# Attention scores scaled in their PSUM bank by the instruction that finds the row's extreme, in a two-group encoder layer

## The chip, the cores and the metric

The kernel runs on 1 core of one Trainium2 chip. The metric is the device time of one execution in microseconds (us), as a median of several runs. A core has a matrix engine (TensorE, PE in the profile; its weight loads are PEld), VectorE (DVE), ScalarE (ACT), GpSimd (POOL) and SyncE (SP). Here SP issues all DMA transfers, in one queue. PSUM is the memory that the matrix engine writes into; a "bank" below is a PSUM tile.

## The reference

Two request groups ("prompt" and "sample", 1024 tokens of 1024 channels each) go through the same layer, one after the other. Only what the change touches is shown: the scores are scaled by 1/8, a softmax is taken over 1024 keys, and at the end a gated residual is added to x.

```python
# branch A: 8 query heads, 2 key heads; branch B: 4 heads, two softmax maps each
qa = rms_norm(qa, qn_a); ka = rms_norm(ka, kn_a)         # per head, then rotary positions
s = einsum('bqgrd,bkgd->bgrqk', qblk, k) * scale         # scale = 1/sqrt(64)
p = softmax(s)                                            # over 1024 keys
oa = (p @ v) * silu(za)
p = softmax(s)                                            # branch B, maps m = 0, 1
pd = p[:, :, 0] - lam * p[:, :, 1]
ob = rms_norm(pd @ v, subln_g) * (1 - lam_init) * silu(zb)
merged = sigmoid(ga) * (oa @ w_proj_a) + sigmoid(gb) * (ob @ w_proj_b)
y = x + gate * (merged @ w_out)
```

The kernel gets x of both groups also transposed (`xT_prompt`, `xT_sample`) and writes y transposed.

## The kernel before

All matrices of weights are split into a high and a low part (`w[..., 0, :]`, `w[..., 1, :]`: ACT at L193 rounds, POOL at L195 subtracts), so a product takes three matmuls. For each group the program runs:

- `kva_gen`, `qa_gen`, `qkb_gen`, `vb_gen`: projections for keys, queries and values. `proj_tt` (L569) fills a bank `f` for a token tile of 128; ACT copies it into `row` (L584), `rms` takes sums of squares (L588, L589 on DVE) and a power of -0.5 (L590 on POOL), `rope` turns the positions (L613 to L619), and L630 transposes the row on PE.
- `z_gen` (L755, L763, L765): the gate paths; it fills PE between attention steps.
- `attention`: 64 units a run, four score tiles each, 256 tiles in all. `scores` calls `softmax_unit` for a tile of 128 queries by 1024 keys. PE writes it into a bank `s` (L789, L790; two 512-wide halves, two matmuls each). DVE takes the negated maximum of the raw row (L791) and multiplies it by `rs` (L792). `rs` is the query's inverse RMS: the queries are left unnormalised, and their norm comes in as the scale of the exponential. ACT then computes exp(rs * s + m) into a tile `p` with the row's sum (L793). `flip` transposes `p` in 32 by 32 blocks on DVE (L834); in branch B it first combines the two maps (L833, with a factor from L818 on DVE and L819 on POOL). Four DMAs bring the pieces to the right partitions of a tile `q` (L843), and `a_values` (L857) or `b_values` (L874) multiplies by the values on PE.
- `gated_gen` (L952, L962 to L964): loads attention outputs (`od`) back and applies the gates.
- `merge_gen` (L1029), then `out_gen` (L1064, L1069) for the first group and `out_seven` (L1136, L1174, a seven-product scheme) for the second. Both load rows of x (L1057, L1115, L1166) and add the product to them.

There are two `s` banks. So a score tile waits until the exponential of the tile two before it has read its bank. There are four `p` tiles and three `q` tiles.

The order on each engine is made at build time: the tile framework schedules all instructions by estimated durations, and steps of the attention get a higher priority (`high_priority(offset=AHEAD)`). The streams are mixed by `weave` with shares such as `Z_SHARE` and `ATT_W`. `behind(a, b)` adds a dependency without a wait: it only puts a after b in the order. An instruction that costs another estimate can therefore change the order of everything that is scheduled after it.

The 1/sqrt(64) of the scores (`SC`) is in the gain tables `gqa` and `gB`, made once (L434, L470).

Of the kernel before, what the change touches and what calls it, by code (L numbers as in the profile page):

```python
# [14 lines left out]
AF = mybir.ActivationFunctionType  # L15
ALU = mybir.AluOpType
# [4 lines left out]
P = 128  # L21
# [68 lines left out]
def kernel(ctx: ExitStack, tc: tile.TileContext, t: dict):  # L90
# [340 lines left out]
    def load_tables():  # L431
        for dst, src in ((gqa, "qn_a"), (gka, "kn_a")):
            dma(dst, t[src][0].partition_broadcast(P))
        nc.vector.tensor_scalar(out=gqa, in0=gqa, scalar1=SC, scalar2=None, op0=ALU.mult)  # L434

# [31 lines left out]
    def load_tables_B():  # L467
        for i, src in enumerate(("qn_b", "kn_b")):
            dma(gB[:, i, :], t[src][0].partition_broadcast(P))
        nc.vector.tensor_scalar(out=gB[:, 0, :], in0=gB[:, 0, :], scalar1=SC, scalar2=None, op0=ALU.mult)  # L470
        nc.vector.tensor_tensor(out=gB[:, 1, 16:], in0=gB[:, 1, 16:], in1=gB[:, 0, 16:], op=ALU.mult)
# [311 lines left out]
    def softmax_unit(q, sw, k, pt, su, rs):  # L783

        m = tiny.tile([P, 1], F32, tag="m", name=nm("m"))
        s = sbank()
        for n in range(2):
            sl = slice(n * 512, (n + 1) * 512)
            nc.tensor.matmul(s[:, sl], q, k[:, sl], start=True, stop=False)  # L789
            nc.tensor.matmul(s[:, sl], sw, k[:, sl], start=False, stop=True)  # L790
        nc.vector.tensor_reduce(out=m, in_=s, axis=AX.X, op=ALU.max, negate=True)  # L791
        nc.vector.tensor_tensor(out=m, in0=m, in1=rs, op=ALU.mult)  # L792
        nc.scalar.activation(  # L793
            pt.rearrange("p (j c a) -> p j c a", j=4, c=8), s.rearrange("p (c a j) -> p j c a", c=8, j=4),
            AF.Exp, bias=m, scale=rs, accum_out=su,
        )
# [137 lines left out]


    def gated_gen(st, i, hf, oT):

# [11 lines left out]
        for c in range(2):  # L949
            e = 2 * i + c  # L950
            o = rtile()
            dma(o, st["od"][e][hf])  # L952
            if e < 4:
# [95 lines left out]
    def out_gen(g, mT):  # L1049

        for eu in range(4):
            w = load_w(w_cols(w_out, (eu * 256, 256)))
            ys = halves(pair())
            for e in range(2):
                ec = eu * 2 + e
                y = ys[e]
                dma(y, xT_in[g][ec * P : (ec + 1) * P])  # L1057
                for hf in range(2):
# [46 lines left out]
    def out_seven(g, parts, md):  # L1105
# [4 lines left out]
        def open_pair(d, job):  # L1110
            job["w"] = load_seven(d)
            job["y"] = [ptile() for _ in range(2)]
            for e in range(2):
                ec = d + 4 * e
                dma(job["y"][e], xT_in[g][ec * P : (ec + 1) * P])  # L1115
            job["t"] = mtile("tab", [P, 512])
# [48 lines left out]
        for e in range(2):  # L1165
            dma(ys[e], xT_in[g][e * 512 : e * 512 + P])  # L1166
        sums = sums_of(parts, md)
# [215 lines left out]
```

## Time and profile before

| | |
|---|---|
| median of 3 runs | 1889.78 us (1889.75 to 1890.94) |
| the profiled execution | 1885.75 us, of which the span is 1884.0 us |
| TensorE busy | 1837.1 us (98% of the span), 10398 matmuls |
| VectorE busy | 1227.3 us (65%) |
| ScalarE busy | 777.3 us (41%) |
| GpSimd busy | 610.7 us (32%) |
| granted TensorE clock | 0.992 of full speed |

The span runs from the first to the last instruction. A group row of the profile gives line, engine, operation, output<-inputs and shapes, then the count, the busy time, the mean duration in ns, the engine's idle time just before these instructions, and what ended it. Matmuls are pipelined and their recorded ends are modelled, so their mean duration (396 ns at L755) is longer than the distance between two of them. A row of waits reads: who waited, for whom, us in total, how many times, the longest.

### The profile page before, as it was taken

The page shows a single profiled execution, that of the slowest core. Times are in us where ns is not written, and L with a number is a line of the kernel's source. Part 1 is how long each engine was busy: PE and PEld are TensorE (multiplying, and loading weights), DVE is VectorE, ACT ScalarE, POOL GpSimd, SP SyncE. Part 2 cuts the span into 40 slices and gives each one's busy share as a digit, 9 for nine tenths or more (in the row PEclk, how much of TensorE's full clock was granted, in tenths as well). Part 3 has the DMA queues.
Part 4 walks back from the last instruction along what each step waited for, and adds up shares of the span by engine and source line. Part 5 has one row for each costly group of instructions (what it writes and reads, how often), then busy time and mean ns, then how long its engine had stood idle before and what let it go on. Part 6 is the DMA issues. An engine that isn't in the chain of part 4 may idle for free.

```text
span 1884.0 us, 29900 instructions
## 1 busy us (share of the span) xinstructions
PE 1837.1 (98%) x10398; PEld 1552.8 (82%) x10398; DVE 1227.3 (65%) x2016; ACT 777.3 (41%) x1544; POOL 610.7 (32%) x888
## 2 busy tenths in 40 slices
PE   6999999999999999999999999999999999999999
PEld 3798878888899877888889887788888898888887
DVE  5777766454776777347466687665357856773795
ACT  4544434343554544213223444344344545442241
POOL 1343311442453452221233333014354635232100
PEclk7999999999999999999999999999999999999999
DMA  9135776564444467754631567666524443675442
GB/s 324 57 94 160 208 197 181 147 181 143 124 113 121 132 205 226 236 154 134 209 134 52 158 180 196 191 183 187 163 72 133 120 117 101 177 245 171 129 129 90
DMA packets 283895, 295.46 MB, mean 157 GB/s; under 512 B 41952, under 2 KB 236640, under 8 KB 283744
## 3 DMA queue, kind: packets, MB, share of 16 engines
q1 hardware_dynamic: 283744, 293.54, 53.1%
q8 instruction: 83, 1.36, 0.3%
q14 instruction: 68, 0.56, 0.1%
HBM read 133.98 MB, written 42.01 MB: 93 GB/s over the span
## 4 chain that ended last, share of the span: by engine, by line
PE 67%; issue 4%; DMA 4%; DVE 3%; POOL 3%; SPq 2%; ACT 1%; ACTq 0%; POOLq 0%; DVEq 0%
PE f L755 16%; PE f L569 14%; PE f L1029 7%; PE a L874 5%; PE s L789 4%; PE s L790 4%; PE a L857 3%; PE s L1029 3%; PE f L1064 3%; PE s L1064 2%; PE f L1136 2%; SPq L843 1%; PE s L1136 1%; DMA q<-p 1%; DMA st<-in_w_in_dram 1%
## 5 line engine op out<-in xcount | busy, mean ns | idle before, releaser
L755 PE MATMUL f<-u,w 128*128 128x512 f32 x2232 | 565.7, 396 | 1.0 <-POOL w L195 0.8
L755 PEld LDWEIGHTS f<-u,w 128*128 128x128 f32 x2232 | 410.5, 189 | 83.8 <-POOL w L195 1.8
L569 PE MATMUL f<-w,u 128*128 128x256 f32 x3456 | 472.7, 287 | 1.8 <-ACT row L584 0.6
L569 PEld LDWEIGHTS f<-w,u 128*128 128x128 f32 x3456 | 449.7, 192 | 23.2 <-issue 3.3
L791 DVE TENSOR_REDUCE m<-s 128x1 f32<-128x1024 f32 x256 | 309.4, 1217 | 104.4 <-PE s L790 102.4
L195 POOL TENSOR_TENSOR w<-st,w 128x512 fp32r<-128x512 f32 x160 | 214.1, 1356 | 394.5 <-ACT w L193 375.6
L834 DVE STREAM_TRANSPOSE p<-p 128x1024 f32<-128x1024 f32 x192 | 237.7, 1242 | 84.3 <-ACT p L793 68.2
L793 ACT ACTIVATE p<-s,m,u 128x1024 f32<-128x1024 f32 x128 | 153.9, 1204 | 164.8 <-issue 71.1
L790 PE MATMUL s<-u,sw 128*128 128x512 f32 x512 | 201.5, 398 | 0.0
L793 ACT ACTIVATE p<-s,m,rsB 128x1024 f32<-128x1024 f32 x128 | 153.8, 1203 | 107.2 <-DVE m L792 88.1
L193 ACT ACTIVATE w<-st 128x512 fp32r<-128x512 f32 x184 | 107.4, 626 | 99.5 <-DMA st<-in_w_in_dram 85.7
L1029 PE MATMUL f<-u,w 128*128 128x512 f32 x552 | 131.1, 392 | 0.0
L874 PE MATMUL a<-q,u 128*128 128x256 f32 x512 | 125.1, 381 | 2.8 <-DMA q<-p 1.9
L857 PE MATMUL a<-q,u 128*64 128x256 f32 x1024 | 117.9, 382 | 5.5 <-DMA q<-p 4.9
L1029 PEld LDWEIGHTS f<-u,w 128*128 128x128 f32 x552 | 103.0, 188 | 21.1
L590 POOL TENSOR_TENSOR rsB<-ss,nhalf 128x4 f32<-128x4 f32 x64 | 65.9, 1031 | 150.9 <-DVE ss L589 132.9
L633 DVE TENSOR_TENSOR u<-f,u 64x256 fp32r<-64x256 f32 (+1 forms) x198 | 81.4, 411 | 48.6 <-ACT u L632 43.3
L763 ACT ACTIVATE ev<-f 128x512 f32<-128x512 f32 x93 | 55.2, 594 | 139.0 <-PE f L755 90.3
L790 PEld LDWEIGHTS s<-u,sw 128*128 128x128 f32 x512 | 96.7, 189 | 16.8 <-issue 0.4
L789 PE MATMUL s<-u 128*128 128x512 f32 x256 | 107.6, 425 | 2.9 <-ACT p L793 2.9
L874 PEld LDWEIGHTS a<-q,u 128*128 128x128 f32 x512 | 94.7, 190 | 17.9 <-issue 3.3
L857 PEld LDWEIGHTS a<-q,u 128*64 128x64 f32 x1024 | 76.3, 137 | 40.0 <-issue 10.3
(221 smaller groups left out, 2181.6 us busy)
## 6 DMA issues: line engine op xcount, KB each, us to landing
q<-p SPq DMA_DIRECT2D x768, 128.0 KB, 2.6
st<-in_w_in_dram SPq DMA_DIRECT2D x132, 256.0 KB, 3.2
zd<-ev SPq DMA_DIRECT2D x96, 256.0 KB, 2.6
sw<-u SPq DMA_DIRECT2D x256, 64.0 KB, 2.0
u<-in_w_ada_dram SPq DMA_DIRECT2D x8, 1024.0 KB, 11.4
oo<-zd SPq DMA_DIRECT2D x64, 128.0 KB, 2.3
od<-oo SPq DMA_DIRECT2D x64, 128.0 KB, 2.4
st<-in_w_in_dram SPq DMA_DIRECT2D x64, 128.0 KB, 2.7
```

Of the source, the lines that this page charges most:

```text
L193: nc.scalar.activation(wh, st, AF.Copy)
L195: e.tensor_tensor(out=wl, in0=st, in1=wh.bitcast(F32), op=ALU.subtract)
L569: ins = nc.tensor.matmul(ps, lt[c][:, sl], w[:, c, wi, :], start=(k == 0), stop=(k == 23))
L755: ins = nc.tensor.matmul(ps, w[:, c, wi, e * P : (e + 1) * P], rt[c], start=(k == 0), stop=(k == 23),)
L789: nc.tensor.matmul(s[:, sl], q, k[:, sl], start=True, stop=False)
L790: nc.tensor.matmul(s[:, sl], sw, k[:, sl], start=False, stop=True)
L791: nc.vector.tensor_reduce(out=m, in_=s, axis=AX.X, op=ALU.max, negate=True)
L793: nc.scalar.activation(pt.rearrange("p (j c a) -> p j c a", j=4, c=8), s.rearrange("p (c a j) -> p j c a", c=8, j=4), AF.Exp, bias=m, scal ...
L834: nc.vector.transpose(pt, pt)
L857: lambda k=k, m=m: nc.tensor.matmul(acc[(LO, HI)[m]], u["v"][:, k], pT[m][:, k], start=(k == 0), stop=(k == 7))
L874: nc.tensor.matmul(acc, u["v"][:, k], pT[:, k], start=(k == 0), stop=(k == 7))
L1029: nc.tensor.matmul(ps, w[:, c, wi, d * P : (d + 1) * P], o[:, oi, :], start=(k == 0), stop=(k == 11))
```

## The change

In `softmax_unit`, one VectorE instruction takes the place of two. It multiplies the bank by `rs` in place, takes the minimum with 3.0e38 (which changes nothing), and gives the row's minimum as an accumulator output. The gain tables carry -SC in place of SC, so the bank holds negated scores and the minimum is the negated maximum. The exponential then has the constant scale -1.0 and only its bias is read for each row.

The second part: rows of x in `out_gen` and `out_seven` are put behind the last load of an attention output in `gated_gen` by `behind`.

```diff
-        nc.vector.tensor_scalar(out=gqa, in0=gqa, scalar1=SC, scalar2=None, op0=ALU.mult)
+        nc.vector.tensor_scalar(out=gqa, in0=gqa, scalar1=-SC, scalar2=None, op0=ALU.mult)
...
-        nc.vector.tensor_scalar(out=gB[:, 0, :], in0=gB[:, 0, :], scalar1=SC, scalar2=None, op0=ALU.mult)
+        nc.vector.tensor_scalar(out=gB[:, 0, :], in0=gB[:, 0, :], scalar1=-SC, scalar2=None, op0=ALU.mult)
...
-        nc.vector.tensor_reduce(out=m, in_=s, axis=AX.X, op=ALU.max, negate=True)
-        nc.vector.tensor_tensor(out=m, in0=m, in1=rs, op=ALU.mult)
+        nc.vector.tensor_scalar(out=s, in0=s, scalar1=rs, scalar2=3.0e38, op0=ALU.mult, op1=ALU.min, accum_out=m)
         nc.scalar.activation(
             pt.rearrange("p (j c a) -> p j c a", j=4, c=8), s.rearrange("p (c a j) -> p j c a", c=8, j=4),
-            AF.Exp, bias=m, scale=rs, accum_out=su,
+            AF.Exp, bias=m, scale=-1.0, accum_out=su,
         )
...
+    rows_in = [None]
...
-            dma(o, st["od"][e][hf])
+            rows_in[0] = dma(o, st["od"][e][hf])
...
-                dma(y, xT_in[g][ec * P : (ec + 1) * P])
+                behind(dma(y, xT_in[g][ec * P : (ec + 1) * P]), rows_in[0])
...
-                dma(job["y"][e], xT_in[g][ec * P : (ec + 1) * P])
+                behind(dma(job["y"][e], xT_in[g][ec * P : (ec + 1) * P]), rows_in[0])
...
-            dma(ys[e], xT_in[g][e * 512 : e * 512 + P])
+            behind(dma(ys[e], xT_in[g][e * 512 : e * 512 + P]), rows_in[0])
```

What this moves in the built program, at three places. Lines after L792 are one less in the changed kernel, and from `gated_gen` on one more.

VectorE at the first score tiles of the run; `s` is the scores' bank, `m` the row's extreme, `u` holds `rs`, `p` is a transposed tile of exponentials. Before:

```order
L791 TENSOR_REDUCE m_1452<-s_1453 128x1
L765 SCALAR_TENSOR_TENSOR ev_1394<-ev_1394,s_1317 128x512
L792 TENSOR_TENSOR m_1452<-m_1452,u_360 128x1
L834 STREAM_TRANSPOSE p_1451<-p_1451 128x1024
L588 TENSOR_REDUCE ss_1417<-row_1414 128x4
L589 TENSOR_SCALAR ss_1417<-ss_1417 128x4
L791 TENSOR_REDUCE m_1462<-s_1463 128x1
L792 TENSOR_TENSOR m_1462<-m_1462,u_360 128x1
L791 TENSOR_REDUCE m_1492<-s_1493 128x1
L792 TENSOR_TENSOR m_1492<-m_1492,u_360 128x1
```

And VectorE at the same place of the changed kernel:

```order
L791 TENSOR_SCALAR s_1453,m_1452<-s_1453,u_360 128x1024
L765 SCALAR_TENSOR_TENSOR ev_1394<-ev_1394,s_1317 128x512
L833 STREAM_TRANSPOSE p_1451<-p_1451 128x1024
L588 TENSOR_REDUCE ss_1417<-row_1414 128x4
L589 TENSOR_SCALAR ss_1417<-ss_1417 128x4
L791 TENSOR_SCALAR s_1462,m_1461<-s_1462,u_360 128x1024
L791 TENSOR_SCALAR s_1491,m_1490<-s_1491,u_360 128x1024
L833 STREAM_TRANSPOSE p_1460<-p_1460 128x1024
```

Nothing stands any more between a tile's pass over the bank and the value that its exponential needs; before, the gate product L765 stood there for the first tile. Over the whole run at least one other instruction stood between L791 and its L792 for 184 of the 256 tiles.

The matrix engine early in branch B of the second group, from the end of one score tile (`s_14308` before, `s_14103` in the changed kernel) on. Before:

```order
L790 MATMUL s_14308<-u_12448,sw_14235 128x512
L569 MATMUL f_14399<-w_14376,u_9120 128x256 x2
L569 MATMUL f_14399<-w_14376,u_9122 128x256
L789 MATMUL s_14340<-u_12447 128x512
L790 MATMUL s_14340<-u_12447,sw_14235 128x512
L789 MATMUL s_14340<-u_12447 128x512
L790 MATMUL s_14340<-u_12447,sw_14235 128x512
L569 MATMUL f_14399<-w_14376,u_9120 128x256 x2
L569 MATMUL f_14399<-w_14376,u_9122 128x256
```

And the matrix engine at the same place of the changed kernel:

```order
L790 MATMUL s_14103<-u_12275,sw_14033 128x512
L630 MATMUL f_13976<-ident,row_13840 128x128 x2
L755 MATMUL f_13953<-u_8995,w_13736 128x512
L755 MATMUL f_13953<-u_8993,w_13736 128x512
L789 MATMUL s_14134<-u_12274 128x512
L790 MATMUL s_14134<-u_12274,sw_14033 128x512
L789 MATMUL s_14134<-u_12274 128x512
L790 MATMUL s_14134<-u_12274,sw_14033 128x512
L789 MATMUL s_14148<-u_12275 128x512
L790 MATMUL s_14148<-u_12275,sw_14033 128x512
```

The third score tile, which reuses the first one's bank, now follows the second at once. Before, 35 matmuls of L569 and seven of L874 stood with the four score matmuls between the first and the third.

SP's queue while branch B of the first group ends; `q<-in_xT_prompt` are rows of x, `row<-od` the loads for the gates, `p<-zd` and `tab<-zd` stored gate paths. Before:

```order
L843 DMA q_7862<-p_7799 128x1x256 x4
L1057 DMA q_8832<-in_xT_prompt_dram 128x1024 x2
L1019 DMA p_8494<-zd_3893 128x512
L1019 DMA p_8494<-zd_4009 128x512
L1019 DMA p_8532<-zd_4806 128x512
L1019 DMA p_8532<-zd_5163 128x512
L768 DMA zd_7817<-ev_7815 128x512
L1057 DMA q_8977<-in_xT_prompt_dram 128x1024 x2
```

And SP's queue of the changed kernel, where these rows of x now stand:

```order
L953 DMA row_8339<-od_137 128x512
L235 DMA st_8523<-in_w_proj_b_dram 128x512
L1058 DMA q_8704<-in_xT_prompt_dram 128x1024 x2
L1016 DMA tab_8264<-zd_7012 128x512
L235 DMA st_8527<-in_w_proj_b_dram 128x512
L1058 DMA q_8849<-in_xT_prompt_dram 128x1024 x2
L1058 DMA q_9026<-in_xT_prompt_dram 128x1024 x2
```

Three pairs of x rows have moved behind the last five loads for the gates and behind stores and weights that stand between. In the second group the rows of x stood behind those loads before, too.

## The prediction

> **What bounds the kernel now.** I read the page's busy shares first, then busy time by stage, then the waits of the matrix engine alone, since it is busy nearly throughout.
>
> ```profile
> PE 1837.1 (98%) x10398; PEld 1552.8 (82%) x10398; DVE 1227.3 (65%) x2016; ACT 777.3 (41%) x1544; POOL 610.7 (32%) x888
> ```
>
> ```profile
> 0.00:100.00 100.00, 77.09 (x462) 59.94 (x463) 68.96 (x171) 47.13 (x109) 27.58 (x33) 0.86 0.53 185
> 100.00:1850.00 1750.00, 1729.82 (x9806) 1468.22 (x9805) 1143.53 (x1825) 728.94 (x1433) 583.13 (x856) 1.00 0.54 157
> 1850.00:1884.00 34.00, 30.20 (x134) 24.68 (x132) 14.83 (x21) 1.23 (x2) 0.00 (x0) 1.00 0.16 62
> ```
>
> The second listing has, for each stretch, its length and the busy time of PE, PEld, DVE, ACT and POOL, then the granted clock. The change alters no matmul, so PE's 1837.1 us stay. PE idles 22.9 us in the first 100 us and 3.8 us at the end. The start keeps its order: the first difference on any engine is at the first score tiles, past 100 us. The end has no scores. That leaves 1750.00 - 1729.82 = 20.2 us of PE's idle time within reach, 1.1% of the time. No saving on VectorE or ScalarE can bring more than that. What ends these waits:
>
> ```profile
> PE f L630 <- POOL row L619: 4.9, 4, 2.2
> PE a L857 <- DMA q<-p: 4.9, 4, 1.6
> PE s L789 <- ACT p L793: 3.7, 4, 1.8
> PE a L874 <- DMA q<-p: 1.9, 2, 1.4
> PE f L630 <- DVE row L619: 1.5, 1, 1.5
> PE a L874 <- DMA sw<-u: 0.9, 1, 0.9
> ```
>
> These rows (100 to 1850 us) sum to 17.8 us. Three kinds matter: 6.8 us for transposed exponentials that come late (q<-p), 6.4 us for projected rows (L630), and 3.7 us for a score bank that its exponential has not yet read (L789).
>
> **The change part by part.** The instructions that it touches, by group:
>
> ```profile
> L791 DVE TENSOR_REDUCE m<-s 128x1 f32<-128x1024 f32 x256 | 309.4, 1217 | 104.4 <-PE s L790 102.4
> L793 ACT ACTIVATE p<-s,m,u 128x1024 f32<-128x1024 f32 x128 | 153.9, 1204 | 164.8 <-issue 71.1 <-DVE m L792 34.8 <-DMA q<-p 25.0
> L792 DVE TENSOR_TENSOR m<-m,rsB 128x1 f32<-128x1 f32 x128 | 28.8, 231 | 1.8
> L792 DVE TENSOR_TENSOR m<-m,u 128x1 f32<-128x1 f32 x128 | 28.0, 224 | 2.7
> L793 ACT ACTIVATION_READ_ACCUMULATOR p<-s,m,u 128x1 f32 x128 | 24.6, 192 | 0.0
> L818 DVE RECIPROCAL r<-su 128x1 f32<-128x1 f32 x64 | 10.3, 160 | 52.4 <-ACT p L793 52.0
> L765 DVE SCALAR_TENSOR_TENSOR ev<-ev,f 128x512 f32<-128x512 f32 x29 | 19.6, 677 | 5.1 <-ACT ev L763 4.7
> L1069 DVE SCALAR_TENSOR_TENSOR q<-f,gatec,q 128x512 f32<-128x512 f32 x9 | 6.7, 746 | 12.9 <-PE f L1064 12.9
> L524 ACT ACTIVATE s<-p 128x1024 f32<-128x1024 f32 x8 | 8.2, 1022 | 7.9 <-DMA p<-in_x_sample_dram 7.9
> ```
>
> Removed on VectorE: the reduction and the small product, (309.4 + 28.8 + 28.0) / 256 = 1439 ns a tile.
>
> Added: one pass over the same 1024 elements, which also writes them back, with a scale read per row. I take the reduction's 1217 ns for the pass. A per-row scale costs 746 - 677 = 69 ns, from two operations of one shape that read a bank, one with such a scale. No row shows VectorE writing a bank. The nearest is ScalarE's L524, which writes 1024 elements into a bank in 1022 ns, less than the 1204 ns of L793 that writes them to the other memory; so I take the write as hidden. The bounds are nothing, and a second pass of 1217 ns. The accumulator output may be an instruction of its own, as ScalarE's is (192 ns); on VectorE I take the smallest operation, 160 ns, with 0 and 192 as ends. The sum is 1217 + 69 + 160 = 1446 ns, 7 ns more than before; over 256 tiles that is +1.8 us of VectorE time, hidden beside PE at 65% busy. The ends are -57 us (neither scale, write nor read costs anything) and about +322 us (a second pass and a 192 ns read).
>
> Here a page bears on the accumulator. The Trainium skill, "VectorE: DVE Perf Modes", section "Two Vector instructions with no wait between them", says that an operation that also writes out its accumulator is two instructions, and its "Rules for kernel authors" advise against fusing for speed, since each operation drains the pipeline and the count is what matters. By these the count stays two for each tile and VectorE gains nothing; without the separate read it would gain 256 x 160 ns = 41 us. No run yet shows which holds.
>
> ScalarE: the exponential loses its per-row scale.
>
> ```profile
> L359 ACT ACTIVATE u<-u,modc x4: 798/806/818, 30.3 to 40.4; 128x512 f32<-128x512 f32 x4
> L416 ACT ACTIVATE u<-u,modc x8: 717/724/730, 63.3 to 70.2; 128x512 f32<-128x512 f32 x8
> ```
>
> L359 reads a scale and a bias for each row, L416 a bias alone: 806 - 724 = 82 ns at the median. So L793 goes to about 1122 ns, or stays at 1204 if the scale is not what these differ by. 256 x 82 ns = 21 us leave an engine that is 41% busy: nothing directly, but each score tile's chain is 0.08 us shorter.
>
> The larger effect is on the wait before the exponential. Until now the extreme became usable only after L792, and the transposes of other tiles could stand between. In branch B, VectorE in order of time (start, duration, instruction):
>
> ```profile
> 629.00 1.22 DVE L791 TENSOR_REDUCE m<-s 128x1 f32<-128x1024 f32 x1
> 630.14 1.23 DVE L834 STREAM_TRANSPOSE p<-p 128x1024 f32<-128x1024 f32 x1
> 631.30 0.67 DVE L792 TENSOR_TENSOR m<-m,rsB 128x1 f32<-128x1 f32 x1
> ```
>
> The reduction ends at 630.22, the product at 631.97, 1.75 us later, with a transpose of 1.23 us between. With one instruction that becomes about 0.23 us (69 + 160 ns): 1.5 us sooner here. Where nothing stands between, nothing is gained. The transpose behind it starts no later, since VectorE's work per tile is the same.
>
> What that is worth on PE: each wait for q<-p is at most 1.6 us, about the size of the gain, and hangs on the exponential. I take 6.5 of the 7.7 us (4.9 + 1.9 + 0.9) off. The L630 waits follow from squares' sums (L588) queued on VectorE behind attention and from POOL behind them; those queues stay as long but regroup. I take half of 6.4 us, 3.2 us. Bounds for both: none of it, and all 14.1 us.
>
> Against it stands the new order: the scheduler now puts score tiles closer together. The second order excerpt shows the worst kind, a third tile right behind the second. Its bank is free only after the chain of the first: fused pass and read 1.45 us, exponential 1.12 us. Hand-overs come from this place in order of time:
>
> ```profile
> 1485.06 0.33 DVE L792 TENSOR_TENSOR m<-m,rsB 128x1 f32<-128x1 f32 x1
> 1485.48 1.20 ACT L793 ACTIVATE p<-s,m,rsB 128x1024 f32<-128x1024 f32 x1 [2.71 <-issue]
> 1486.82 0.50 PE L789 MATMUL s<-u 128*128 128x512 f32 x1 [1.05 <-ACT p L793]
> ```
>
> 0.09 us to ScalarE and 0.14 us back to PE; the whole chain is 2.8 us when nothing is in its way. Between the first and the third tile of the excerpt PE has six 512-wide matmuls and two transposes:
>
> ```profile
> 1793.16 2.72 PE s L1029 x12
> 650.55 0.22 PE f L630 x2
> ```
>
> That is 6 x 0.227 + 0.22 = 1.58 us of work, 1.2 us short. Counted so over the whole order, eight tiles in the changed kernel have less than 3.0 us of PE work before their bank is wanted (before: one). They fall 4.7 us short of 2.8 us in all. I add 4.7 us to the 3.7 us paid now; the ends are 0, if the delayed matmuls only use up a later wait, and +11 us, below.
>
> Rows of x: they are moved behind five gate loads, and behind the weights and stored gates between them.
>
> ```profile
> L1057 SPq DMA_DIRECT2D q<-in_xT_prompt_dram x8: 333/476/825, 761.2 to 910.5; - x8
> L1057 SPq EVENT_SEMAPHORE  x3: 17/28/28, 761.1 to 910.1; - x3
> L1069 DVE SCALAR_TENSOR_TENSOR q<-f,gatec,q x9: 736/745/752, 891.6 to 973.6; 128x512 f32<-128x512 f32 x9
> ```
>
> The first x rows are issued at 761 us and used from 891.6 us on, and their longest wait in the queue is 28 ns, so they held up no gate load. Moved later by at most some tens of us they stay early. Price 0 both ways; the cover is the first 512-wide products L1029 ahead of L1064. If that cover were used up, the add L1069 would be late, not PE at first.
>
> The sum: -6.5 - 3.2 + 4.7 + 0 = -5.0 us. It is made against the profiled execution (1885.75 us, span 1884.0). The median of the runs, 1889.78 us, is 4 us above that, and I carry the difference over to it: 1884.8 us.
>
> **The rivals.**
>
> Same: the waits change places. For it speaks that PE's idle time is 1.1% and that the matmul order is redrawn almost everywhere, so old waits go and others of like size come. Against it, every removed queue entry shortens the path to PE. Time 1889.8 us.
>
> Slower: the score banks. The chain of 2.8 us holds only if VectorE is free when the scores are done. If it takes 3.8 us, one transpose of 1.2 us in the way less a little, 15 places fall short, by 14.7 us in all; minus the 3.7 us of now that is +11 us: 1900.8 us with nothing gained elsewhere. It decides from a chain of about 3.5 us. A wait can also cost more than itself:
>
> ```profile
> 746.33 0.50 PE L789 MATMUL s<-u 128*128 128x512 f32 x1 [1.80 <-ACT p L793]
> 746.00:750.00 4.00, 3.67 (x11) 2.97 (x12) 1.99 (x3) 1.95 (x5) 0.34 (x1) 0.71 0.90 298
> ```
>
> After that wait the granted clock is 0.71 over the next 4 us, so (1 - 0.71) x 4 = 1.2 us are lost once more. The Trainium skill, "TensorE: Matmul & The Clock Gate", section "Part 1: The HAM clock gate (the "warmup" mystery)", has the clock halved only after an idle window of about 3.4 us. By that page no wait of this length would cost extra, by this row some do.
>
> Much slower: the pass that writes into the bank it reads takes a second pass's time. The chain is then 4.0 us and VectorE goes to (1227.3 + 312) / 1884 = 82%. Bank waits alone come to +14 us, queues on VectorE would add about as much: 1910 us or more. Only L524 speaks against it.
>
> Much faster: nearly all 17.8 us go: 1872 us. The closer score tiles speak against it.
>
> **How the numbers follow.** 0.2% (3.8 us) is about what a measurement of this kernel can tell from no change. Forecast, faster by about 5 us with its own range of 1874 to 1886: 0.40; much faster 0.05; same 0.25; slower by banks 0.24; much slower 0.06. Hence faster 0.45, same 0.25, slower 0.30. The range of 1873 to 1902 us leaves out the last case, the extreme of much faster and the end of the bank case.
>
> **What would show it.** In the changed profile: L791 as a pass of about 1.29 us and perhaps a read of about 0.16 us, VectorE's busy sum within 30 us of 1227; L793 at 1.12 us; in PE's waits q<-p under 2 us, L789 between 4 and 10 us, PE's idle time between 100 and 1850 us near 15 us. I am wrong if PE's idle time grows, with L789 on L793 as its largest row, if the pass is near 2.4 us, or if L857 and L874 still wait as long, which would say that the transposes and the DMAs behind them, not the exponential, were late.

## The result and the profile after

The changed kernel takes 1900.78 us (median of 4 runs, 1899.79 to 1901.77), the kernel before 1889.76 us beside it (4 runs, 1889.55 to 1890.94): ratio 1.0059, 95% interval 1.0047 to 1.0072. It is 11 us slower; the forecast was 1884.8 us and faster. The profiled execution took 1901.36 us with a span of 1899.6 us.

First the page's busy sums and the groups of the changed instructions, in the form of the rows shown of before:

```profile
PE 1845.7 (97%) x10398; PEld 1551.6 (82%) x10398; DVE 1203.5 (63%) x2016; ACT 761.5 (40%) x1544; POOL 614.9 (32%) x888
...
L792 ACT ACTIVATE p<-s,m 128x1024 f32<-128x1024 f32 x256 | 285.1, 1114 | 266.4 <-DVE s L791 207.0
...
L791 DVE TENSOR_SCALAR_CACHE_REDUCE s<-s,u 128x1024 f32<-128x1024 f32 x128 | 163.4, 1288 | 87.6 <-PE s L790 86.6
...
L791 DVE TENSOR_SCALAR_CACHE_REDUCE s<-s,rsB 128x1024 f32<-128x1024 f32 x128 | 163.3, 1285 | 53.2 <-PE s L790 52.6
```

The instructions came out at the sizes forecast: the pass 1286 to 1288 ns, the exponential 1114 ns. All lines from L793 to L931 stand one lower than before. VectorE and ScalarE are both less busy (by 23.8 and 15.8 us). PE, with the same 10398 matmuls, is busy 8.6 us longer.

The same change seen on L791 alone (count, then shortest, median and longest duration in ns):

```profile
L791 DVE TENSOR_SCALAR_CACHE_REDUCE s<-s,u x128: 1253/1292/1295, 128.9 to 1350.2; 128x1024 f32<-128x1024 f32 x128
L791 DVE DVE_READ_ACCUMULATOR s<-s,u x128: 82/141/145, 130.1 to 1351.4; 128x1 f32 x128
```

The accumulator is read by an instruction of its own, 82 to 145 ns.

Now PE in the middle stage (length, then busy time of PE, PEld, DVE, ACT and POOL, then the granted clock), and what ended its waits between 100 and 1866 us (total, times, longest):

```profile
100.00:1866.00 1766.00, 1739.28 (x9812) 1467.54 (x9812) 1120.54 (x1827) 713.07 (x1433) 588.66 (x856) 0.99 0.54 156
```

```profile
PE s L789 <- ACT p L792: 10.4, 9, 4.3
PE a L873 <- DMA st<-in_w_in_dram: 3.8, 1, 3.8
PE f L569 <- POOL w L195: 2.9, 4, 1.0
PE f L569 <- ACT w L193: 2.5, 3, 1.2
PE f L630 <- POOL row L619: 1.7, 4, 0.8
PE f L630 <- DVE row L619: 1.4, 1, 1.4
...
PE a L873 <- DMA q<-p: 0.6, 1, 0.6
```

PE idles 26.7 us in the middle stage, 20.2 us before. One of the old waits shrank as forecast: L630 went from 6.4 to 3.1 us. Bank waits (L789) rose from 3.7 to 10.4 us, and new ones came: 5.4 us on L569 for rounded weights (0.4 us before). The row of 3.8 us on L873 names a weight transfer, but these matmuls read `q` and the values, no weights. SP and PE at this place, in order of time (start, duration, instruction):

```profile
683.69 2.18 SPq L842 DMA_DIRECT2D q<-p  x2
685.97 1.25 SPq L217 DMA_DIRECT2D st<-in_w_in_dram  x2
688.97 3.61 PE L873 MATMUL a<-q,u 128*128 128x256 f32 x9 [3.84 <-DMA st<-in_w_in_dram]
```

The weight transfers issued from 685.97 on take 3.6 us to land, so they land after the matmul has started. The last transfer of transposed exponentials, issued at 685.3 us, also takes 3.6 us and lands just before the start. So the matmul waited for q<-p under another transfer's name. The same holds for the 1.0 us on L873 that the profile names oo<-zd. In the run with the pass alone, below, the wait at this place bears its right name:

```profile
PE a L873 <- DMA q<-p: 3.2, 1, 3.2
```

By landing times q<-p costs 0.6 + 3.8 + 1.0 = 5.4 us, 6.8 us before.

The longest of the bank waits, with what each engine did, from the three engines' time lines (start, duration, instruction):

```profile
1510.30 0.79 PE L789 MATMUL s<-u 128*128 128x512 f32 x1 [4.33 <-ACT p L792]
```

```profile
1505.83 1.29 DVE L791 TENSOR_SCALAR_CACHE_REDUCE s<-s,rsB 128x1024 f32<-128x1024 f32 x1
```

```profile
1508.53 0.63 ACT L193 ACTIVATE w<-st 128x512 fp32r<-128x512 f32 x1 [2.13 <-DMA st<-in_w_in_dram]
1509.06 1.10 ACT L792 ACTIVATE p<-s,m 128x1024 f32<-128x1024 f32 x1
```

The pass for the tile is over at 1507.1 us. Its exponential starts at 1509.06, because in ScalarE's queue a weight rounding stands ahead of it, which itself waits 2.13 us for its transfer. PE pays 4.33 us, and then the clock is lower, as shown below. Two shorter waits stand at another place on PE:

```profile
1181.77 0.50 PE L789 MATMUL s<-u,u 128*128 128x512 f32 x1 [1.21 <-ACT p L792]
...
1184.17 0.38 PE L569 MATMUL f<-w,u 128*128 128x256 f32 x1 [1.20 <-ACT w L193]
```

Stretches of 3.4 us around both places (length, PE, PEld, DVE, ACT, POOL busy, granted clock):

```profile
1181.10:1184.50 3.40, 1.53 (x5) 0.86 (x5) 3.34 (x6) 2.14 (x5) 0.31 (x1) 1.00 0.70 199
1184.50:1187.90 3.40, 2.43 (x9) 2.19 (x9) 2.96 (x5) 1.92 (x4) 0.96 (x1) 0.50 0.75 201
...
1505.40:1508.80 3.40, 0.57 (x6) 0.45 (x4) 3.30 (x7) 1.20 (x3) 3.40 (x7) 0.99 0.39 106
1508.80:1512.20 3.40, 1.90 (x5) 1.41 (x6) 0.34 (x2) 2.55 (x5) 2.58 (x6) 0.50 0.75 206
```

After a stretch in which PE was busy 1.53 of 3.40 us the granted clock is 0.50 in the next. In the span the 6.5 us of added idle time in the middle and the 8.6 us of added busy time nearly make up the 15.6 us between the two spans. These are two single executions. Whether the lower clock is a price of the change they can't tell: in the profile of one pass in the old order, below, PE is busy nearly as long.

### The profile page after: what moved, and what is told of

Same layout as the page of the kernel before. It is cut to its first block, busy times and chain, and to the rows that moved or that the text cites. A ratio compares the mean times of both kernels' runs of the same rounds, so it can differ in the third digit from the quotient of the medians.

```text
span 1899.6 us, 29840 instructions
## 1 busy us (share of the span) xinstructions
PE 1845.7 (97%) x10398; PEld 1551.6 (82%) x10398; DVE 1203.5 (63%) x2016; ACT 761.5 (40%) x1544; POOL 614.9 (32%) x888
## 4 chain that ended last, share of the span: by engine, by line
PE 82%; DVE 4%; DMA 4%; POOL 3%; issue 2%; ACT 2%; SPq 2%; DVEq 0%; POOLq 0%; ACTq 0%
PE f L755 22%; PE f L569 19%; PE f L1030 7%; PE a L856 6%; PE s L789 5%; PE s L790 5%; PE a L873 5%; PE s L1030 3%; PE f L1065 3%; PE s L1065 2%; PE f L1137 2%; SPq L842 1%; PE s L1137 1%; DMA st<-in_w_in_dram 1%; POOL w L195 1%
## 5 line engine op out<-in xcount | busy, mean ns | idle before, releaser
L755 PE MATMUL f<-u,w 128*128 128x512 f32 x2232 | 573.9, 396 | 1.6 <-DVE ssB L886 1.2
L569 PE MATMUL f<-w,u 128*128 128x256 f32 x3456 | 482.8, 288 | 6.6 <-POOL w L195 2.9
L569 PEld LDWEIGHTS f<-w,u 128*128 128x128 f32 x3456 | 454.3, 194 | 27.9 <-POOL w L195 3.7
L792 ACT ACTIVATE p<-s,m 128x1024 f32<-128x1024 f32 x256 | 285.1, 1114 | 266.4 <-DVE s L791 207.0
L195 POOL TENSOR_TENSOR w<-st,w 128x512 fp32r<-128x512 f32 x160 | 216.9, 1374 | 400.0 <-ACT w L193 313.0
L791 DVE TENSOR_SCALAR_CACHE_REDUCE s<-s,u 128x1024 f32<-128x1024 f32 x128 | 163.4, 1288 | 87.6 <-PE s L790 86.6
L791 DVE TENSOR_SCALAR_CACHE_REDUCE s<-s,rsB 128x1024 f32<-128x1024 f32 x128 | 163.3, 1285 | 53.2 <-PE s L790 52.6
L193 ACT ACTIVATE w<-st 128x512 fp32r<-128x512 f32 x184 | 107.9, 626 | 101.4 <-DMA st<-in_w_in_dram 88.1
L873 PE MATMUL a<-q,u 128*128 128x256 f32 x512 | 127.0, 384 | 5.4 <-DMA st<-in_w_in_dram 3.8
L1030 PE MATMUL f<-u,w 128*128 128x512 f32 x552 | 131.1, 392 | 0.0
L789 PE MATMUL s<-u 128*128 128x512 f32 x256 | 106.5, 418 | 7.9 <-ACT p L792 7.9
L873 PEld LDWEIGHTS a<-q,u 128*128 128x128 f32 x512 | 95.3, 192 | 20.5 <-DVE u L633 4.3
L584 ACT ACTIVATE row<-f 128x256 f32<-128x256 f32 (+1 forms) x112 | 41.2, 368 | 161.4 <-PE f L569 155.9
```

The lines of the kernel that those rows point to most:

```text
L193: nc.scalar.activation(wh, st, AF.Copy)
L195: e.tensor_tensor(out=wl, in0=st, in1=wh.bitcast(F32), op=ALU.subtract)
L569: ins = nc.tensor.matmul(ps, lt[c][:, sl], w[:, c, wi, :], start=(k == 0), stop=(k == 23))
L755: ins = nc.tensor.matmul(ps, w[:, c, wi, e * P : (e + 1) * P], rt[c], start=(k == 0), stop=(k == 23),)
L791: nc.vector.tensor_scalar(out=s, in0=s, scalar1=rs, scalar2=3.0e38, op0=ALU.mult, op1=ALU.min, accum_out=m)
L792: nc.scalar.activation(pt.rearrange("p (j c a) -> p j c a", j=4, c=8), s.rearrange("p (c a j) -> p j c a", c=8, j=4), AF.Exp, bias=m, scal ...
```

## Experiments

Four theories were on trial. A: the new order puts score tiles closer together, and PE pays for the banks. B: the pass itself costs, in any order. C: in the new order weights come late behind a full SP queue (the expectations count the 3.8 us on L873 for this, though it was a wait for q<-p). D: weights come late in the new order whatever the queue does, PE waits for them, and exponentials stand behind roundings that wait. Except for two edits of the source (the rows of x), kernels were made in the *finished order*: the scheduler lays the program out, and then single instructions are replaced, removed or moved, with their waits, while the rest keeps its order. The placeholder, below, is an edit of the source and of the finished order. "New order" is the changed kernel's, "old order" that of the kernel before. Several kernels of one group ran beside the same runs of the kernel before, whose median went from 1885.86 to 1889.98 us over the groups; so ratios are compared across groups, and times within one.

### Which part costs: the order, the pass or the rows of x

One pass in the old order:

```diff
 # finished order of the kernel before
-DVE TENSOR_REDUCE m <- s
+DVE TENSOR_SCALAR s,m <- s,rs        (in the reduction's place)
-DVE TENSOR_TENSOR m <- m,rs
-ACT ACTIVATE p <- s,m  scale=rs
+ACT ACTIVATE p <- s,m  scale=-1.0    (waits for the pass)
```

> The instructions of the changed kernel in the order of the kernel before: every engine issues what it issued before and in that row, but the one pass stands where the reduction stood, the small product is gone, and the exponential waits for the pass and has the constant scale. Theory (the new order costs the time, the new instruction does not): 1884 to 1891 us, at or a little under before, since the chain from scores to the end of the exponential is about 0.8 us shorter in the mean. Rival (the pass itself costs the time, by writing the bank or by its longer hold of VectorE): 1897 to 1904 us, as the changed kernel.

Measured: 1887.88 us, ratio 0.9990, 0.9976 to 1.0003 (median, ratio to the kernel before, 95% interval of the ratio).

The two steps back in the new order:

```diff
 # finished order of the changed kernel
-DVE TENSOR_SCALAR s,m <- s,rs
+DVE TENSOR_REDUCE m <- s
+DVE TENSOR_TENSOR m <- m,rs          (right behind it)
-ACT ACTIVATE p <- s,m  scale=-1.0
+ACT ACTIVATE p <- s,m  scale=rs
```

> The mirror image: the order of the changed kernel on every engine, but with the reduction and the small product back to back in place of the one pass, and the exponential scaled per row again. Theory (order): 1898 to 1908 us, no faster than the changed kernel. Rival (the pass itself): 1887 to 1893 us, back at the time before.

Measured: 1910.31 us, ratio 1.0114, 1.0087 to 1.0142, just above the range of the order theory.

The rows of x alone, in the source of the kernel before:

```diff
-dma(y, xT_in[g][ec * P : (ec + 1) * P])
+behind(dma(y, xT_in[g][ec * P : (ec + 1) * P]), rows_in[0])
```

> The kernel before with the rows of x bound behind the gate loads and nothing else. Theory (the binding is worth nothing, since these loads never waited): 1888 to 1892 us. Rival (the binding delays the first group's end, which came 4.6 us later in the changed kernel): 1893 to 1897 us.

Measured: 1885.34 us, ratio 0.9990, 0.9972 to 1.0007. The time lies below both ranges, but the ratio can't be told from 1.

The pass alone, the changed kernel's source without that edit:

```diff
-behind(dma(y, xT_in[g][ec * P : (ec + 1) * P]), rows_in[0])
+dma(y, xT_in[g][ec * P : (ec + 1) * P])
```

> The changed kernel without the binding of the rows of x. Its order differs from that of the changed kernel in a few places only. Theory: 1899 to 1903 us, the same as the changed kernel. Rival (the binding costs some of the 11 us): 1890 to 1897 us.

Measured: 1900.81 us, ratio 1.0061, 1.0041 to 1.0081. PE's busy sum and waits of the pass in the old order, and below the waits of the two steps in the new order (100 to 1866 us):

```profile
PE 1844.7 (98%) x10398; PEld 1556.0 (82%) x10398; DVE 1207.6 (64%) x2016; ACT 756.6 (40%) x1544; POOL 610.4 (32%) x888
...
PE f L630 <- POOL row L619: 5.2, 5, 2.2
PE a L874 <- DMA q<-p: 3.2, 2, 2.4
PE a L874 <- DMA zd<-ev: 2.1, 1, 2.1
PE f L630 <- DVE ss L589: 1.8, 1, 1.8
PE a L857 <- DMA q<-p: 1.8, 3, 0.6
```

```profile
PE s L789 <- ACT p L792: 13.4, 10, 4.6
PE a L873 <- DMA st<-in_w_in_dram: 4.4, 1, 4.4
...
PE a L856 <- DMA q<-p: 1.8, 3, 0.9
PE f L630 <- DVE row L619: 1.5, 1, 1.5
PE f L630 <- POOL row L619: 1.3, 3, 0.5
...
PE a L873 <- DMA q<-p: 0.8, 1, 0.8
```

The rows of x do nothing that can be measured. The pass does nothing in the old order that could be measured and gains some 10 us in the new one. In the old order 255 separate wait instructions of 21 ns stand ahead of the passes, 18 ahead of the small products before; what they cost is not known, and the pass may be worth more there than measured. The new order costs 20.3 us with the two steps (1910.31 against 1889.98 us) and 12.9 us with the pass (1900.81 against 1887.88 us). The loss is the order's.

PE is busy 1844.7 us in the profile of one pass in the old order, 7.6 us more than before and 1.0 us less than in the changed kernel, though its median time is that of the kernel before. The mean granted clock is 0.986 in both profiles and 0.992 in that of before. (The profiled execution, 1892.72 us, was the slowest of its ten.) So the longer busy time at half clock is not shown to be a price of the new order.

### The same work in an order closer to the old one

```diff
 nc.vector.tensor_scalar(out=s, in0=s, scalar1=rs, ..., accum_out=m)
+nc.vector.tensor_tensor(out=m, in0=m, in1=rs, op=ALU.mult)   # seen by the scheduler,
+                                                             # deleted from the finished order
```

> The changed kernel, laid out by the scheduler with a small VectorE product behind each pass (so that it spaces the score tiles about as in the kernel before); the product is then deleted from the finished order, so the work that runs is that of the changed kernel. Score tiles with less than 3.0 us of PE work between tile n's scores and tile n+2's: 3 (changed kernel 14, kernel before 4). Theory A (the closer score tiles cost the time): 1882 to 1889 us, PE's waits for the exponential on L789 under 3 us (changed kernel 10.4). Theory B (the pass in place itself costs, by longer waits whatever the order): 1895 to 1902 us, L789 waits still near 10 us. If it falls between, 1890 to 1895, the spacing is part of it and another part of the order costs as well.

Measured: 1888.18 us, ratio 0.9997, 0.9980 to 1.0014. PE's bank wait in it:

```profile
PE s L789 <- ACT p L793: 1.4, 3, 0.5
```

With the scheduler told of the small product, and the product then gone, the loss is gone too. There is no gain over the kernel before either. Its order has no more than three close score tiles by the count above, but other things differ in it as well, so this alone does not show that closeness was the cause.

### Is it the chain from scores to free bank?

The pass over fewer columns takes about 1.0 us out of the chain, in both orders; the scaling and the extreme of the other 960 columns are left out:

```diff
-DVE TENSOR_SCALAR s,m <- s,rs   128x1024
+DVE TENSOR_SCALAR s,m <- s,rs   128x64
-ACT ACTIVATE p <- s,m  scale=-1.0
+ACT ACTIVATE p <- s,rs scale=0.0     (same size)
```

> The changed kernel in its finished order, with the pass cut from 1024 to 64 columns (the other columns' scaling and extreme are left out, and the exponential takes the row scale as its bias and 0 as its scale, so its own work stays as it is). It takes about 1.1 us out of the chain from scores to free bank, and some 290 us of VectorE's work. Theory A (bank waits behind closer score tiles): PE's waits on L789 fall from 10.4 to under 3 us and the time from 1900.8 to 1886 to 1893 us. Theory C (late weights behind a full SP queue, L569 and L873, with the bank waits only in their wake): 1896 to 1901 us, with L569 and L873 waits together still over 7 us. The twin in the old order tells what the lighter VectorE is worth by itself.

> The order of the kernel before with the one pass in the reduction's place, and the same cut of the pass from 1024 to 64 columns (the rest of its work left out, as in the twin). One pass in the old order took 1887.9 us with L789 waits of 0.6 us. Theory A (bank waits belong to the new order): 1882 to 1888 us, a gain of at most 6 us, less than half of what the twin gains. A rival (VectorE's load holds PE in both orders alike): the gain is as large as the twin's, 8 us or more, 1880 us or less.

Measured: new order 1895.41 us, ratio 1.0042, 1.0028 to 1.0056; old order 1880.39 us, ratio 0.9967, 0.9949 to 0.9986. PE's waits in the new order with the short pass:

```profile
PE s L789 <- ACT p L792: 7.6, 6, 4.3
```

Both times lie between the ranges of their theories. Both orders seem to gain (0.17% against the changed kernel, 0.23% against one pass in the old order, each about as large as its uncertainty), and the order's price stays: 15.0 us (1895.41 against 1880.39 us). The longest bank wait stays at 4.3 us. So this microsecond of the chain from scores to a free bank is not what the orders differ by, and my theory A fell in its first form.

### Is it the weights' place on the queue?

```diff
 # finished order, SP's queue: a weight transfer goes ahead of up to 4 right before it
-q<-p  q<-p  q<-p  q<-p  st<-in_w_in_dram
+st<-in_w_in_dram  q<-p  q<-p  q<-p  q<-p
```

> The changed kernel in its finished order but for SP's queue: each weight transfer (st<-in_w_in_dram) goes ahead of up to 4 transfers of the attention (q<-p, od<-oo, oo<-zd) that stand right before it; 92 of 200 move, 69 of them by 4 places, about 0.6 us of issue each. Theory C (in the new order weights come late, PE waits for their rounding on L569, and exponentials queue behind roundings on ScalarE): PE's waits on L569 for w fall from 5.4 to under 2 us, the wait of 3.8 us on L873 goes, and the time falls from 1900.8 to 1888 to 1895 us. Theory A (bank waits behind closer score tiles): L789 stays near 10 us and the time at 1898 to 1903 us. A rival (the order of the matmuls itself, with q<-p late in place of weights): 1898 us or more, and the waits on q<-p (0.6 us) grow by what L569 loses.

> The same on SP in the order of the kernel before, with the one pass in the reduction's place (1887.9 us without the move); 82 weight transfers move. Theory C: weights were not late in this order, so 1885 to 1890 us, q<-p waits (5.0 us) up by 0 to 3 us. A rival (early weights help any order): 1882 us or less.

> The changed kernel's order with both cuts: the pass over 64 of the 1024 columns (the rest of it left out, the exponential with the row scale as bias and 0 as scale) and the weight transfers up to 4 places earlier on SP. The short pass alone took 1895.4 us in this order, 1880.4 us in the old one. If late weights are what is left of the order's price, 1880 to 1888 us. If the weight transfers are not it, 1893 to 1897 us, as with the short pass alone.

Measured: new order 1941.30 us, ratio 1.0278, 1.0243 to 1.0313; old order 1934.51 us, ratio 1.0242, 1.0209 to 1.0275; the new order with the short pass as well 1931.90 us, ratio 1.0227, 1.0199 to 1.0255. All three are far slower than the theories had it; only the open-ended rival of the first (1898 us or more) has the time, and its sign, waits on q<-p that grow by what L569 loses, did not come. PE's waits in the new order, then SP's wait for a free staging buffer in this kernel and in the changed one:

```profile
PE a L873 <- DMA q<-p: 25.3, 5, 6.0
...
PE f L569 <- ACT w L193: 2.5, 3, 1.2
PE f L569 <- POOL w L195: 2.4, 3, 1.0
```

```profile
SPq L217 <- POOL w L195: 97.9, 60, 9.5
```

```profile
SPq L217 <- POOL w L195: 61.6, 48, 9.5
```

The waits on L569 stayed (4.9 us, from 5.4). So moving the transfers ahead brought no weights sooner. They wait on SP for GpSimd to finish with the staging buffer (97.9 us, from 61.6), and the transposed exponentials that now stand behind them came late. This edit did more than move transfers, however: it makes each transfer wait by name for the one eight places before it, and the profile counts 30123 instructions where the changed kernel has 29840. What part of the 40 us these waits cost was not measured. The form of theory C that blamed the queue found no support, but it was not tested by itself.

### Is it that PE wants weights before they are ready?

The roundings read data that lies ready, in place of the transfer:

```diff
-ACT ACTIVATE     w_hi <- st          (waits for the transfer of st)
+ACT ACTIVATE     w_hi <- identity    (doesn't)
-POOL TENSOR_TENSOR w_lo <- st, w_hi
+POOL TENSOR_TENSOR w_lo <- identity, w_hi
+ # waits that these had implied are added by name where a tile's place is still in transfer
```

> The changed kernel in its finished order; the roundings of w_in (L193 on ScalarE, L195 on GpSimd and VectorE) read the identity, which lies ready, in place of the transferred weights and don't wait for the transfer; the transfers themselves go as before (so the products are not those of the reference). Theory D (in the new order exponentials stand behind roundings that wait for weights on ScalarE, and PE waits for the rounded weights): ScalarE's waits for st (84.9 us) go, PE's waits on L789 fall from 10.4 to under 4 us and those on L569 for w from 5.4 to under 1.5 us, and the time falls from 1900.8 to 1886 to 1892 us. A rival (the order on PE itself, whatever the weights do): 1896 us or more. Its twin in the old order tells what ready weights are worth in any order.

> The same in the order of the kernel before with the one pass in the reduction's place (1887.9 us without). Theory D: 1884 to 1888 us, a gain of at most 4 us, so that the price of the new order over the old one falls from 12.9 to under 5 us. The rival: both gain alike and the price stays at 9 us or more.

Measured: new order 1894.30 us, ratio 1.0040, 1.0024 to 1.0055, between the range of theory D and that of its rival; old order 1893.13 us, ratio 1.0032, 1.0015 to 1.0049. That the old order became slower was expected by no theory, and the added waits were the suspect. So two controls carry these waits alone, and a third run puts ready weights into the order of the placeholder:

```diff
 # finished order, as the changed kernel (or one pass in the old order) but for
+ # waits by name for transfers that still read or write a tile's place
```

> Control: the changed kernel in its finished order with only the added waits of the ready-weights runs (transfers that still read or write a tile's place are waited for by name, which other waits had implied). If the added waits cost nothing: 1899 to 1902 us. If they cost what the old order's twin lost (5.2 us): 1905 to 1908 us, and then ready weights are worth some 11 us in the new order in place of 6.5.

> The same control in the order of the kernel before with one pass (1887.9 us without). If the added waits cost nothing: 1886 to 1890 us, and the 5.2 us that ready weights cost there are the roundings' own doing, which start earlier. If the waits cost it: 1892 to 1895 us, and ready weights are worth nothing in the old order.

> Ready weights (w_in's roundings read the identity and don't wait for the transfer, so the products are not the reference's) in the order that the scheduler gave with a placeholder behind the pass, 1888.2 us without. Theory D (late weights are what the new order pays for): 1885 to 1893 us, so that the new order's 1894.3 us stands at most 9 us off; with a gain here as large as in the new order (6.5 us, 1882 us or less) late weights are no matter of the order, and its price stays 12 us.

Measured: new order with the waits alone 1907.90 us, ratio 1.0116, 1.0101 to 1.0131; old order 1900.93 us, ratio 1.0076, 1.0047 to 1.0105; ready weights in the placeholder's order 1894.53 us, ratio 1.0045, 1.0029 to 1.0062. The first is in the range for waits that cost something; the second is slower than both its ranges, and the third 1.5 us slower than theory D's. PE's waits with ready weights in the new order, and in the control:

```profile
PE s L789 <- ACT p L792: 9.5, 9, 2.5
...
PE f L569 <- POOL w L195: 0.4, 1, 0.4
```

```profile
PE s L789 <- ACT p L792: 12.6, 9, 4.2
...
PE f L569 <- POOL w L195: 3.2, 5, 1.0
PE f L569 <- ACT w L193: 2.6, 2, 1.4
```

By the ratios the added waits cost 0.55% (10 us) in the new order and 0.86% (16 us) in the old one. Against its control, ready weights gain 0.76% (14 us) in the new order and 0.44% (8 us) in the old one. The order's price is 12.9 us without the waits, 7.0 us with them (1907.90 against 1900.93 us) and 1.2 us with ready weights on top; all three orders then lie within 0.13% of each other (1.0032 to 1.0045). The fall from 7.0 to 1.2 us is not clear of the noise: the ratio of the old order's control is known to 0.3% (5.5 us) either way. The placeholder's order had no control with the waits alone.

Theory D also named its own signs. PE's waits for rounded weights went as it said (0.4 us, from 5.4). The bank waits were to fall under 4 us and stayed at 9.5 us; only the longest fell, from 4.2 to 2.5 us. ScalarE's waits for weight transfers hardly differ (L193 on st<-in_w_in over the whole run: 85.7 us before, 88.1 us in the changed kernel). So late weights may be part of the order's price, but that they are is not shown, and exponentials behind waiting roundings do not account for the bank waits as a whole. The added waits cost the old order more than the new one and may hide part of the price.

### Is it the closeness of score tiles on PE?

```diff
 # finished order of the changed kernel, PE's queue alone
-scores n-2, scores n-1, scores n, L569 or L755 or ...
+scores n-2, scores n-1, L569 or L755 or ..., scores n
```

> The changed kernel in its finished order but for PE's queue: where a tile's four score matmuls would start with less than 3.6 us of PE work behind the scores of two tiles before, they go behind up to 2.6 us of the matmuls that follow (18 places); the work and the other engines' orders are those of the changed kernel. Theory A (closer score tiles on PE, whatever holds up their exponentials): L789 falls from 10.4 to under 4 us and the time from 1900.8 to 1889 to 1894 us. Theory D (late weights): L569's waits for w stay over 4 us and the time at 1897 to 1901 us, as what PE no longer waits for on L789 it waits for on the weights. Half of each: 1894 to 1897 us.

> The same with 4.0 us in place of 3.6 us (31 places). Theory A: as the run with 3.6 us or up to 3 us below it, 1886 to 1892 us. Theory D: 1897 us or more, no better than with 3.6 us.

Measured: 1910.79 us (3.6 us apart), ratio 1.0112, 1.0091 to 1.0133; 1915.88 us (4.0 us apart), ratio 1.0144, 1.0122 to 1.0167. PE's waits with 3.6 us, then the bank wait with 4.0 us:

```profile
PE f L630 <- POOL row L619: 10.2, 5, 3.5
PE f L569 <- ACT w L193: 5.6, 2, 3.3
...
PE f L569 <- POOL w L195: 4.2, 6, 1.0
PE s L789 <- ACT p L792: 3.0, 3, 2.1
...
PE f L630 <- DVE row L619: 1.4, 1, 1.4
```

```profile
PE s L789 <- ACT p L792: 1.4, 2, 0.8
```

The bank waits went, from 10.4 to 3.0 and 1.4 us, and the time rose, by 0.5 and 0.8% (10 and 16 us). The matmuls that now stand where PE waited for a bank wait in turn: on weights 9.8 us (5.4 in the changed kernel), on projected rows 11.6 us on both rows of L630 (3.1). More closeness taken away costs more. The first time is above the ranges of both theories; the second is where theory D had it (1897 us or more). Theory A fell in its second form too: the bank waits can go and the time does not fall. The edit also issues the moved scores later, and with them all that follows from them, so it does not price the bank waits alone. In these orders a wait for a bank was mostly followed by others that took its place.

## Why the prediction was wrong, point by point

**Sizes of instructions: right.** The pass was put at 1217 + 69 ns and took 1286 to 1288 ns, which fits a write into the bank that is hidden, and the second pass of the much slower rival did not occur. The read was put at 160 ns; it takes 82 to 145 ns. VectorE was to stay within 30 us and lost 23.8 us. One sum of the forecast was off, without effect: (309.4 + 28.8 + 28.0) / 256 is 1430 ns, not 1439, so its own figures add 16 ns a tile and 4.0 us in all, not 7 ns and 1.8 us. The exponential was put at 1122 ns and takes 1114 ns. The Trainium skill, "VectorE: DVE Perf Modes", section "Two Vector instructions with no wait between them", has an operation that writes out its accumulator as two instructions; the trace agrees, 128 + 128 reads of 82 to 145 ns.

**Rows of x: right.** Put at 0; alone they measured 0.9990, 0.9972 to 1.0007.

**"I take 6.5 of the 7.7 us" for q<-p: failed.** The prediction let these waits hang on the exponential, which would now end sooner. By landing times q<-p costs 6.8 us before and 5.4 us in the changed kernel. One pass in the old order has 7.1 us (3.2 + 2.1 + 1.8; the row named zd<-ev is q<-p too, since that transfer lands after the matmul's start), and the two steps in the new order have 7.0 us (4.4 + 1.8 + 0.8). The shorter chain took at most 1.4 us off. That L857 and L874 still wait as long was one of the prediction's own signs of being wrong.

**"Half of 6.4 us" for L630: right in the rows, for another reason.** It shrank by 3.3 us, but the two steps in the new order have 2.8 us as well (1.5 + 1.3), and the pass in the old order has more than before (5.2 + 1.8 on two rows). So the new order took this wait off, not the pass.

**"I add 4.7 us" for the new order: the step that turned the sign.** It priced the order by one kind of wait, a score bank that is not free. That term was low by 2.0 us: L789 rose by 6.7 us. (It counted eight close tiles, one before; the expectation for the placeholder counts 14, four before, by the same limit of 3.0 us. Why the two counts differ is not known.) Left out was that everything else on PE was reordered as well: PE waits 5.4 us on L569 for rounded weights in the changed kernel, 0.4 us before, and no term of the sum stands for that. With the gain on q<-p mostly gone and these waits added, PE's idle time rose by 6.5 us where the sum had it fall by 5.0 us. What in the order costs the 13 to 20 us is not settled by these rows: taking the largest of them away did not bring the time back.

**"The change alters no matmul, so PE's 1837.1 us stay": not so in the profile.** PE was busy 8.6 us longer in the changed kernel's profiled execution, with a granted clock of 0.50 after new waits. I had the row for it (0.71 after 746.33) and put it into a rival as 1.2 us, not into the sum. But one pass in the old order shows 7.6 us more as well, at the time of the kernel before, so this is no measure of what the new order costs. The Trainium skill, "TensorE: Matmul & The Clock Gate", section "Part 1: The HAM clock gate (the "warmup" mystery)", asks for an idle window of about 3.4 us. Here the half clock followed a window of 3.4 us with PE busy 1.53 us, so such a window need not be idle throughout; the prediction had held the page against the length of single waits.

**The rival with 1900.8 us** had the right time by luck. It was to be decided by a chain of 3.8 us in place of 2.8 us, and by 11 us more of bank waits with nothing gained elsewhere; the bank waits rose by 6.7 us. Taking 1.0 us out of the chain left the order's price at 15.0 us, and moving scores apart took the bank waits away and made the kernel slower.

**What would show me wrong** was named rightly: PE's idle time grew, with L789 as its largest row. But that the largest row is the cause was my reading, and the runs with scores moved apart speak against it.

**What stays open:** what in the new order costs the time. Neither a microsecond off the chain to a free bank nor scores further apart brought it back. Late weights fit the runs but are not shown. The transfers' place on SP was only tried together with added waits, and neither GpSimd's L195, which frees the staging buffers, nor ScalarE's L193, which stands ahead of exponentials, was moved by itself.

## What to carry to other kernels

Where instructions are laid out by estimated durations, a cheaper instruction is two changes: run it in the old order, and run the old instruction in the new order, before anything is read from the waits; here the pass was worth nothing measurable or 10 us and the order cost 13 to 20 us. If the order is the loss, a placeholder that the scheduler sees and the program drops can give a better order (here 1888.2 against 1900.8 us). On an engine with an in-order queue and 1% of idle time, the largest wait row names what was late first, not what the time hangs on: test it by taking away that wait, and look at what it turns into. Where a wait names a transfer that the instruction does not read, compare the landing times before building on the name: here 3.8 us put down to weights were a wait for q<-p. And an edit of a finished order that adds waits needs a control with the waits alone.

## What the runs showed of the hardware that was not expected

- A pass over 128x64 in the bank, without the read behind it, is far from 1/16 of one over 128x1024 (in the short-pass run, new order; shortest, median, longest in ns):

```profile
L791 DVE TENSOR_SCALAR_CACHE_REDUCE s<-s,u x128: 253/292/295, 127.1 to 1351.0; 128x64 f32<-128x64 f32 x128
```

  With 1292 ns for 1024 columns (medians), a straight line through the two gives an estimate of 1.04 ns a column and some 225 ns that don't depend on the columns.
- In the changed kernel's profile the granted clock fell to 0.50 for 6.8 us after a window of 3.4 us in which PE was busy 1.53 us, with no wait over 1.21 us in it.
- Waits that other waits were meant to imply are not free: added by name they cost 10 us in one order and 16 us in the other. The profiles count 193 and 175 instructions more for them (30033 against 29840, 30312 against 30137). How these cost that much was not looked into.
